# Two-layer decoder trunk on one core: where the norm between two parts is computed, and how the next part's weight splits queue around it

## The chip, the core and the metric

The kernel runs on one core of a Trainium2 chip, in one launch. The metric is device microseconds of that core, the median of several runs. The core has TensorE (PE, with its weight loads PEld), VectorE (DVE), ScalarE (ACT), GpSimd (POOL) and the DMA queue of SyncE (SP), each of which works through its own instructions in order.

## The reference, cut to what matters

The trunk has six parts in a row. Each normalizes its input, computes something with large weights, normalizes the result and adds it to x:

```python
def rmsnorm(x, g):
    y = x * lax.rsqrt(jnp.mean(x * x, -1, keepdims=True) + EPS)
    return y * g

def macaron_half_ffn(x, pre_g, post_g, w_gate, w_up, w_down):
    h = rmsnorm(x, pre_g)
    h = (jax.nn.silu(h @ w_gate) * (h @ w_up)) @ w_down
    return x + 0.5 * rmsnorm(h, post_g)

for p in layers:                       # two layers
    x = macaron_half_ffn(x, *p["ffn1"])
    x = x + rmsnorm(p["mixer"](rmsnorm(x, pre_g), *p["mix"]), post_g)
    x = macaron_half_ffn(x, *p["ffn2"])
```

x is 256 tokens by 1024 channels, float32; the FFN is 2816 wide. The mixer of layer 0 is sparse attention with a short convolution, that of layer 1 a recurrent time mixing.

## The kernel before, in words

Tokens lie on the 128 partitions, so x is two tiles, m = 0 (tokens 0 to 127) and m = 1. Every float32 product is made of three matmuls of rounded pieces (`mm3`, L265 to L270): an operand is split into a high piece (a copy on ACT) and a low piece (source minus high, on DVE or POOL). Weights are loaded by SP into one of four `raw` buffers and split by `split_u` (L214 to L233): the high piece of 128x1024 on ACT at L227, the low piece at L232 on DVE, or, for every `share`-th piece, in two halves of 128x512 on POOL. The pieces lie in 18 buffers `u`, two to a piece.

Each part ends in `out_proj` (L336 to L390). TensorE first finishes the output of m = 0 in two halves of 512 channels; `post_norm` (L317) takes each half: a Square with its row sum on ACT (L326), a multiplication by the gain on DVE (L328), and after the second half `rstd` (L273): the two sums and the epsilon are added on DVE (L276), the power -1/2 is taken on POOL (L277), and DVE adds the scaled halves to x (L331). Then `after(0)` starts the next part for m = 0: `pre_norm` (L282) makes the squares of x on ACT (L288), x times the gain (L290) on POOL for m = 0 and on DVE for m = 1, again `rstd`, and the multiplication by its result on DVE (L293). Eight transposes on TensorE (L300) follow, and `hT_split` splits what they give (L211 on ACT, L212 on DVE). The first FFN of all has no gain at this place (it multiplies later), so L290 isn't in it.

While this chain runs for m = 0, TensorE works on the output of m = 1: 15 of its last 16 steps of three matmuls may go ahead of the transposes of m = 0, the last step may not (`PIN`, L381). Then TensorE has the next part's first matmuls on m = 0, and behind them the transposes of m = 1, whose chain ran in the meantime.

The order within each engine is not written out: a scheduler that simulates the program orders the traced instructions and inserts waits. `issue_after(i)` adds one constraint to that: what is traced inside it stays behind instruction i on i's engine. The five ends of a part are called here A (first FFN to layer 0's mixer), B (that mixer to the second FFN), C (second FFN to the third), D (third FFN to layer 1's mixer) and E (that mixer to the last FFN).

The change touches `split_u`, `rstd`, `pre_norm` and `post_norm`. The three lines of the code that a sentence can't say so well:

```python
(nc.vector if m else nc.gpsimd).tensor_tensor(xg[:, sl], self.x[m][:, sl], g[:, sl], op=ALU.mult)      # L290
nc.vector.scalar_tensor_tensor(r, ss[0], eps, ss[1], op0=ALU.add, op1=ALU.add)                        # L276
nc.gpsimd.tensor_tensor(r2, r, self.nhalf, op=ALU.pow)                                                # L277
```

Of the kernel before, what the change touches and what calls it, by code (L numbers as in the profile page):

```python
# [8 lines left out]
F32 = mybir.dt.float32  # L9
F32R = mybir.dt.float32r  # L10
AF = mybir.ActivationFunctionType
ALU = mybir.AluOpType
# [3 lines left out]
P = 128  # L16
# [5 lines left out]
EPS = 1e-6  # L22
# [7 lines left out]
class Trunk:  # L30
# [31 lines left out]
    def __init__(self, tc, A, es):  # L62
        self.tc, self.nc, self.A = tc, tc.nc, A
        pool = lambda name, bufs, **kw: es.enter_context(tc.tile_pool(name=name, bufs=bufs, **kw))
        self.const = pool("const", 1)
        self.nlo = 0
        self.lead = None
        self.raws = pool("raws", 4)
        self.up = pool("up", 18)
        self.bp = pool("bp", 8)  # L70
        self.xp = pool("xp", 4)
        self.small = pool("small", 1)
        self.gains = pool("gains", 2)
        self.ps_mm = pool("ps_mm", 4, space=PSUM)
        self.ps_fl = pool("ps_fl", 2, space=PSUM)
        self.ps_tr = pool("ps_tr", 2, space=PSUM)
        self.ident = self.const.tile([P, P], F32, name="ident")
        make_identity(self.nc, self.ident)
        self.nhalf = self.const.tile([P, 1], F32, name="nhalf")
        self.nc.vector.memset(self.nhalf, -0.5)  # L80
        self.x = [self.const.tile([P, D], F32, name=f"x{m}") for m in range(2)]


# [128 lines left out]
        return self.nc.vector.tensor_sub(lo, src, hi.bitcast(F32))  # L212

    def split_u(self, src):  # L214
        n = src.shape[1]
        hi, lo = (self.u(F32R)[:, :n * src.shape[2]].rearrange("p (a b) -> p a b", a=n) for _ in range(2))
        self.nlo += 1
        if n == 1 and src.shape[2] == 512:

            if self.nlo % 3 == 0:  # L220
                self.nc.vector.tensor_copy(hi, src)
                self.nc.gpsimd.tensor_sub(lo, src, hi.bitcast(F32))
            else:
                self.split(src, hi, lo)
            return hi, lo
        pool = self.share and self.nlo % self.share == 0
        self.nc.scalar.activation(hi, src, AF.Copy)  # L227
        ax = 1 if n > 1 else 2
        m = src.shape[ax] // (2 if pool else 1)
        for i in range(0, src.shape[ax], m):  # L230
            c = (slice(None),) * ax + (slice(i, i + m),)
            (self.nc.gpsimd if pool else self.nc.vector).tensor_sub(lo[c], src[c], hi[c].bitcast(F32))  # L232
        return hi, lo  # L233
# [36 lines left out]
        mm(out, a[1], b[0], start=False, stop=stop)  # L270


    def rstd(self, ss, eps):  # L273
        nc = self.nc
        r, r2 = self.sm("rstd", 1, bufs=8), self.sm("rstd2", 1, bufs=8)
        nc.vector.scalar_tensor_tensor(r, ss[0], eps, ss[1], op0=ALU.add, op1=ALU.add)  # L276
        nc.gpsimd.tensor_tensor(r2, r, self.nhalf, op=ALU.pow)  # L277
        return r2

    HALF = (slice(0, 512), slice(512, 1024))  # L280

    def pre_norm(self, m, g=None):  # L282
        nc = self.nc
        xn, xg = self.xn(), self.x[m] if g is None else self.xn()
        ss = []
        for sl in self.HALF:
            ss.append(self.sm("ss", 1, bufs=8))
            nc.scalar.activation(xn[:, sl], self.x[m][:, sl], AF.Square, scale=1.0 / 32, accum_out=ss[-1])  # L288
            if g is not None:
                (nc.vector if m else nc.gpsimd).tensor_tensor(xg[:, sl], self.x[m][:, sl], g[:, sl], op=ALU.mult)  # L290
        r = self.rstd(ss, EPS)
        for sl in self.HALF:
            nc.vector.tensor_scalar(xn[:, sl], xg[:, sl], r, None, op0=ALU.mult)  # L293
        return xn
# [22 lines left out]
    def post_norm(self, m, g, half):  # L317

        nc = self.nc
        c = 0.5 if half else 1.0  # L320
        t, sq, ss = self.xn(), self.xn(), []

        def take(b):
            sl = self.HALF[len(ss)]
            ss.append(self.sm("ss", 1, bufs=8))
            nc.scalar.activation(sq[:, sl], b, AF.Square, scale=1.0 / (32 * c), accum_out=ss[-1])  # L326
            r = self.rstd(ss, EPS / (c * c)) if len(ss) == 2 else None
            nc.vector.tensor_mul(t[:, sl], b, g[:, sl])  # L328
            if r is not None:
                for sl in self.HALF:  # L330
                    nc.vector.scalar_tensor_tensor(self.x[m][:, sl], t[:, sl], r, self.x[m][:, sl],  # L331
                                                   op0=ALU.mult, op1=ALU.add)
        return take
# [1176 lines left out]
```

## Time and profile before

| what | value |
|---|---|
| runs | 1164.0, 1166.74, 1168.51 us (median 1166.74) |
| the profiled execution's own time | 1168.6 us |
| its span, first to last instruction | 1166.9 us |
| mean granted TensorE clock | 0.974 |
| busy: PE, DVE, ACT, POOL | 94%, 60%, 51%, 38% of the span |

The span is 1.7 us shorter than the time of the same execution, and that time lies 1.9 us above the median of the runs. A granted clock of 1.0 is 2.4 GHz, 0.5 is 1.2 GHz. A timeline row gives the start, the duration, engine, line, operation, what is written and read, and in brackets how long the engine had been idle and what ended that. Where a row says x2 or x4, several instructions in a row are merged.

### The profile page before, as it was taken

The numbers are of one execution on the slowest core, as the hardware profiler recorded it, in microseconds if no ns is written. First come the engines' busy times: TensorE is split into PE (matmuls) and PEld (weight loads), VectorE is DVE, ScalarE is ACT, GpSimd is POOL, SyncE is SP. The second block draws the span as 40 slices with busy tenths as digits, with TensorE's granted clock in tenths as the row PEclk, the third lists the DMA queues.
The fourth block names the chain that finished last, engine by engine and source line by source line (L and its number), as shares of the span: only waits on it lengthen the run. The fifth ranks groups of instructions, "written<-read, shape, count | busy, mean of one in ns | idle before, by whom it ended". The sixth has DMA issues, their size and how long they took to land. (4 is left out here: it accounts for less than half of the span.)

```text
span 1166.9 us, 16783 instructions
## 1 busy us (share of the span) xinstructions
PE 1098.3 (94%) x6429; PEld 924.2 (79%) x6429; DVE 705.3 (60%) x1165; ACT 594.4 (51%) x1106; POOL 446.3 (38%) x400
## 2 busy tenths in 40 slices
PE   6999998999979999998999999987889798999997
PEld 5888886888958888887888888776548776888886
DVE  5655525656886555427655543889894886655531
ACT  6655544245745555434655532557644454655540
POOL 3523234232563332324432433334463644432331
PEclk9999999999999999999999999999997888999999
DMA  9765562542464665555656563442312234765530
GB/s 324 253 216 180 182 212 64 166 145 73 152 207 154 215 210 182 181 179 180 196 168 196 182 201 106 145 145 73 108 37 92 92 129 142 227 205 179 182 108 36
DMA packets 130749, 187.46 MB, mean 161 GB/s; under 512 B 6871, under 2 KB 101087, under 8 KB 130670
## 3 DMA queue, kind: packets, MB, share of 16 engines
q1 hardware_dynamic: 130670, 186.41, 49.0%
q8 instruction: 50, 0.82, 0.3%
q14 instruction: 29, 0.24, 0.1%
HBM read 185.34 MB, written 1.05 MB: 160 GB/s over the span
## 5 line engine op out<-in xcount | busy, mean ns | idle before, releaser
L232 POOL TENSOR_TENSOR u<-raw,u 128x512 fp32r<-128x512 f32 x222 | 322.2, 1473 | 489.1 <-ACT u L227 476.1
L227 ACT ACTIVATE u<-raw 128x1024 fp32r<-128x1024 f32 x312 | 327.7, 1058 | 283.3 <-PE mm L269 79.7
L232 DVE TENSOR_TENSOR u<-raw,u 128x1024 fp32r<-128x1024 f32 x201 | 276.7, 1381 | 212.4 <-ACT u L227 211.9
L404 PE MATMUL mm<-b,u 128*128 128x512 f32 x504 | 181.3, 398 | 0.0
L404 PE MATMUL fl<-b,u 128*128 128x512 f32 x504 | 180.7, 397 | 0.0
L405 PE MATMUL fl<-b,u 128*128 128x256 f32 x504 | 141.5, 281 | 0.0
L405 PE MATMUL mm<-b,u 128*128 128x256 f32 x504 | 141.4, 280 | 0.0
L270 PE MATMUL fl<-u,b 128*128 128x512 f32 (+1 forms) x304 | 120.0, 396 | 4.8 <-DVE b L212 4.2
L268 PE MATMUL fl<-u,b 128*128 128x512 f32 (+1 forms) x304 | 120.5, 399 | 2.5 <-DVE u L780 1.4
L269 PE MATMUL fl<-u,b 128*128 128x512 f32 (+1 forms) x304 | 120.2, 395 | 1.5 <-DVE u L232 1.5
L268 PE MATMUL mm<-u,b 128*128 128x512 f32 (+1 forms) x296 | 114.8, 389 | 0.2 <-ACT u L211 0.2
L269 PE MATMUL mm<-u,b 128*128 128x512 f32 (+1 forms) x296 | 113.1, 384 | 1.1 <-DVE u L212 0.9
L270 PE MATMUL mm<-u,b 128*128 128x512 f32 (+1 forms) x296 | 112.5, 382 | 0.0
L404 PEld LDWEIGHTS fl<-b,u 128*128 128x128 f32 x504 | 94.9, 188 | 19.7
L404 PEld LDWEIGHTS mm<-b,u 128*128 128x128 f32 x504 | 94.8, 188 | 19.7
L405 PEld LDWEIGHTS mm<-b,u 128*128 128x128 f32 x504 | 95.2, 189 | 3.4
L405 PEld LDWEIGHTS fl<-b,u 128*128 128x128 f32 x504 | 95.2, 189 | 3.1
L270 PEld LDWEIGHTS fl<-u,b 128*128 128x128 f32 x304 | 58.9, 194 | 17.8 <-DVE b L212 4.8
L268 PEld LDWEIGHTS fl<-u,b 128*128 128x128 f32 x304 | 59.0, 194 | 16.2 <-ACT b L211 2.2
L269 PEld LDWEIGHTS fl<-u,b 128*128 128x128 f32 x304 | 59.0, 194 | 13.2 <-DVE u L232 1.7
L268 PEld LDWEIGHTS mm<-u,b 128*128 128x128 f32 (+1 forms) x296 | 55.9, 190 | 12.4 <-issue 1.1
L269 PEld LDWEIGHTS mm<-u,b 128*128 128x128 f32 (+1 forms) x296 | 55.9, 190 | 12.3 <-DVE u L212 1.2
(312 smaller groups left out, 1834.4 us busy)
## 6 DMA issues: line engine op xcount, KB each, us to landing
raw<-in_l_ffn_w_up_dram SPq DMA_DIRECT2D x44, 1024.0 KB, 5.3
raw<-in_l_ffn_w_down_dram SPq DMA_DIRECT2D x44, 1024.0 KB, 5.0
raw<-in_l_ffn_w_gate_dram SPq DMA_DIRECT2D x42, 1024.0 KB, 5.2
raw<-in_l_w_in_dram SPq DMA_DIRECT2D x9, 1024.0 KB, 6.8
raw<-in_l_w_v_dram SPq DMA_DIRECT2D x6, 1024.0 KB
raw<-in_l_w_out_dram SPq DMA_DIRECT2D x4, 1024.0 KB
raw<-in_l_w_r_dram SPq DMA_DIRECT2D x4, 1024.0 KB, 5.2
raw<-in_l_w_k_dram SPq DMA_DIRECT2D x4, 1024.0 KB, 5.2
```

The costliest lines, as they stand in the source:

```text
L227: self.nc.scalar.activation(hi, src, AF.Copy)
L232: (self.nc.gpsimd if pool else self.nc.vector).tensor_sub(lo[c], src[c], hi[c].bitcast(F32))
L268: mm(out, a[0], b[0], start=start, stop=False)
L269: mm(out, a[0], b[1], start=False, stop=False)
L270: mm(out, a[1], b[0], start=False, stop=stop)
L404: mm(b2, w[k][0], x, start=k == 0, stop=False)
L405: mm(b2[:, 0], w[k][1], x[:, 0], start=False, stop=False)
```

## The change

For m = 0 the multiplication of x by its gain goes to DVE too. The two halves' sums are added on ACT, as an Identity activation of the second sum whose bias is the first; the epsilon is added to the first sum on DVE as soon as that sum is there. This holds for both norms and both m. After the norm of m = 0 the last square (ACT), the last multiplication by the gain (DVE) and the power (POOL) are noted, and the weight splits traced after it, from the fifth piece on, must stay behind these three on their engines. Two small constants are set at the start and read by nothing.

```diff
+        self.tail_of, self.held, self.free = {}, [], 0
...
     def split_u(self, src):
+        self.free -= 1
+        with ExitStack() as es:
+            for i in self.held if self.free < 0 else ():
+                es.enter_context(self.tc.issue_after(i))
+            return self.split_free(src)
+
+    def split_free(self, src):
         n = src.shape[1]
...
-    def rstd(self, ss, eps):
+    def rstd(self, ss):
         nc = self.nc
         r, r2 = self.sm("rstd", 1, bufs=8), self.sm("rstd2", 1, bufs=8)
-        nc.vector.scalar_tensor_tensor(r, ss[0], eps, ss[1], op0=ALU.add, op1=ALU.add)
-        nc.gpsimd.tensor_tensor(r2, r, self.nhalf, op=ALU.pow)
+        nc.scalar.activation(r, ss[1], AF.Identity, bias=ss[0])
+        self.tail_of["pow"] = nc.gpsimd.tensor_tensor(r2, r, self.nhalf, op=ALU.pow).ins
         return r2
+
+    def sum_in(self, ss, sq, src, scale, eps):
+        s = self.sm("ss", 1, bufs=8)
+        i = self.nc.scalar.activation(sq, src, AF.Square, scale=scale, accum_out=s)
+        if not ss:
+            e = self.sm("sse", 1, bufs=8)
+            self.nc.vector.tensor_scalar(e, s, eps, None, op0=ALU.add)
+            s = e
+        ss.append(s)
+        return i
...
         for sl in self.HALF:
-            ss.append(self.sm("ss", 1, bufs=8))
-            nc.scalar.activation(xn[:, sl], self.x[m][:, sl], AF.Square, scale=1.0 / 32, accum_out=ss[-1])
+            self.tail_of["sq"] = self.sum_in(ss, xn[:, sl], self.x[m][:, sl], 1.0 / 32, EPS).ins
             if g is not None:
-                (nc.vector if m else nc.gpsimd).tensor_tensor(xg[:, sl], self.x[m][:, sl], g[:, sl], op=ALU.mult)
-        r = self.rstd(ss, EPS)
+                self.tail_of["xg"] = nc.vector.tensor_tensor(xg[:, sl], self.x[m][:, sl], g[:, sl], op=ALU.mult).ins
+        r = self.rstd(ss)
+        if m == 0 and g is not None:
+            self.held, self.free = list(self.tail_of.values()), 4
...
-            ss.append(self.sm("ss", 1, bufs=8))
-            nc.scalar.activation(sq[:, sl], b, AF.Square, scale=1.0 / (32 * c), accum_out=ss[-1])
-            r = self.rstd(ss, EPS / (c * c)) if len(ss) == 2 else None
+            self.sum_in(ss, sq[:, sl], b, 1.0 / (32 * c), EPS / (c * c))
+            r = self.rstd(ss) if len(ss) == 2 else None
```

## Rows read from the trace of the kernel before

**Rows 1.** The profile page, busy time of an engine, its share of the span and its instructions.
```profile
PE 1098.3 (94%) x6429; PEld 924.2 (79%) x6429; DVE 705.3 (60%) x1165; ACT 594.4 (51%) x1106; POOL 446.3 (38%) x400
```

**Rows 2.** The waits of PE over the whole span: who waited for whom, us in total, how often, the longest.
```profile
PE tr L300 <- DVE xn L293: 16.1, 8, 5.2
...
PE fl L270 <- DVE b L212: 4.2, 2, 2.3
```

**Rows 3.** Windows: length, busy time (and instructions) of PE, PEld, DVE, ACT and POOL, granted clock, DMA share and GB/s. The first five run from the last matmul on m = 0's output to the last transpose of m = 1, for the ends A, C, B, D and E; the last four are the stretches of granted clock 0.5 in A, B, C and E.
```profile
187.27:215.29 28.02, 23.80 (x113) 19.25 (x111) 21.31 (x29) 14.48 (x31) 15.59 (x13) 0.94 0.62 177
526.29:555.46 29.17, 26.10 (x113) 20.64 (x111) 22.41 (x26) 14.34 (x26) 12.44 (x10) 0.94 0.54 180
336.02:363.66 27.64, 22.08 (x97) 17.79 (x95) 20.38 (x24) 13.94 (x25) 12.70 (x10) 0.88 0.52 169
718.92:739.69 20.77, 20.77 (x108) 16.12 (x107) 15.45 (x32) 7.24 (x20) 9.81 (x9) 1.00 0.03 5
957.47:987.22 29.75, 25.76 (x109) 20.72 (x107) 21.03 (x26) 15.70 (x27) 15.33 (x12) 0.89 0.51 167
205.13:208.54 3.41, 3.41 (x10) 2.63 (x9) 3.35 (x6) 0.70 (x3) 1.80 (x3) 0.50 1.05 290
345.08:351.91 6.83, 3.59 (x12) 2.96 (x13) 6.16 (x6) 1.67 (x3) 3.90 (x3) 0.50 0.62 197
543.05:546.46 3.41, 3.41 (x10) 2.65 (x9) 3.41 (x6) 0.00 (x0) 0.55 (x1) 0.50 0.94 311
969.72:976.55 6.83, 5.62 (x17) 4.50 (x18) 6.29 (x8) 3.66 (x6) 2.28 (x3) 0.50 0.53 167
```

**Rows 4.** The timelines of PE, DVE, ACT and POOL in end B, engine by engine.
```profile
348.00 1.09 PE L300 MATMUL tr<-ident,xn 128*128 128x128 f32 x4 [5.25 <-DVE xn L293]
...
337.78 2.46 DVE L331 SCALAR_TENSOR_TENSOR x<-xn,rstd,x 128x512 f32<-128x512 f32 x2
340.15 2.32 DVE L232 TENSOR_TENSOR u<-raw,u 128x1024 fp32r<-128x1024 f32 x1
342.39 1.23 DVE L276 SCALAR_TENSOR_TENSOR rstd<-ss 128x1 f32<-128x1 f32 x1
...
346.37 2.89 DVE L293 TENSOR_SCALAR xn<-xn,rstd 128x512 f32<-128x512 f32 x2 [0.45 <-POOL rstd L277]
...
340.27 0.63 ACT L288 ACTIVATE xn<-x 128x512 f32<-128x512 f32 x1 [0.74 <-DVE x L331]
...
337.94 3.44 POOL L232 TENSOR_TENSOR u<-raw,u 128x512 fp32r<-128x512 f32 x2 [0.20 <-ACT u L227]
341.35 3.49 POOL L290 TENSOR_TENSOR xn<-x,gain 128x512 f32<-128x512 f32 x2
344.79 1.54 POOL L277 TENSOR_TENSOR rstd<-rstd,nhalf 128x1 f32<-128x1 f32 x1
```

**Rows 5.** The timelines of PE, DVE and POOL in end E.
```profile
970.61 1.08 PE L300 MATMUL tr<-ident,xn 128*128 128x128 f32 x4 [3.66 <-DVE xn L293]
...
960.29 2.46 DVE L331 SCALAR_TENSOR_TENSOR x<-xn,rstd,x 128x512 f32<-128x512 f32 x2
...
966.09 1.21 DVE L232 TENSOR_TENSOR u<-raw,u 128x1024 fp32r<-128x1024 f32 x1
...
968.98 2.89 DVE L293 TENSOR_SCALAR xn<-xn,rstd 128x512 f32<-128x512 f32 x2 [1.08 <-POOL rstd L277]
...
963.87 4.57 POOL L290 TENSOR_TENSOR xn<-x,gain 128x512 f32<-128x512 f32 x2
968.39 0.56 POOL L277 TENSOR_TENSOR rstd<-rstd,nhalf 128x1 f32<-128x1 f32 x1
```

**Rows 6.** The timeline of DVE in end C (the first four rows) and in end A (the last two).
```profile
528.04 1.42 DVE L331 SCALAR_TENSOR_TENSOR x<-xn,rstd,x 128x512 f32<-128x512 f32 x2
529.37 4.56 DVE L232 TENSOR_TENSOR u<-raw,u 128x1024 fp32r<-128x1024 f32 x2
...
534.66 2.93 DVE L293 TENSOR_SCALAR xn<-xn,rstd 128x512 f32<-128x512 f32 x2 [0.66 <-POOL rstd L277]
...
541.97 0.68 DVE L212 TENSOR_TENSOR b<-tr,b 128x512 fp32r<-128x512 f32 x1
...
197.66 2.88 DVE L293 TENSOR_SCALAR xn<-xn,rstd 128x512 f32<-128x512 f32 x2 [0.46 <-POOL rstd L277]
...
203.93 1.28 DVE L212 TENSOR_TENSOR b<-tr,b 128x512 fp32r<-128x512 f32 x2
```

**Rows 7.** Durations of one instruction: line L290 on POOL and on DVE (ns: least, median, most), and the group of ACT's smallest plain activations (us in all, mean ns).
```profile
L290 POOL TENSOR_TENSOR xn<-x,gain x10: 1267/1912/2318, 191.5 to 966.1; 128x512 f32<-128x512 f32 x10
L290 DVE TENSOR_TENSOR xn<-x,gain x10: 625/685/689, 208.4 to 981.1; 128x512 f32<-128x512 f32 x10
...
L960 ACT ACTIVATE pk<-pk 128x8 f32<-128x8 f32 x3 | 0.7, 227 | 0.1
```

**Rows 8.** The chain of m = 1 in ends A and C: windows (columns as in Rows 3) from the last matmul on m = 1's output to the first transpose of m = 1, and the multiplications on DVE that release these transposes.
```profile
201.95:214.25 12.30, 10.39 (x49) 8.71 (x49) 9.21 (x18) 3.76 (x9) 4.61 (x5) 0.86 1.06 290
539.00:554.42 15.42, 12.91 (x48) 9.87 (x48) 10.66 (x16) 3.72 (x9) 3.05 (x3) 0.89 0.79 270
...
210.41 0.88 DVE L293 TENSOR_SCALAR xn<-xn,rstd 128x512 f32<-128x512 f32 x2 [0.67 <-POOL rstd L277]
...
549.44 0.88 DVE L293 TENSOR_SCALAR xn<-xn,rstd 128x512 f32<-128x512 f32 x2 [0.66 <-POOL rstd L277]
```

More of the change, by code (lines that the diff above doesn't have):

```diff
@@ L80, in __init__ @@
         self.nc.vector.memset(self.nhalf, -0.5)
+        self.epsc = {}
+        for e in (EPS, EPS / (0.5 * 0.5)):
+            self.epsc[e] = self.const.tile([P, 1], F32, name="eps")
+            self.nc.vector.memset(self.epsc[e], e)
+        self.tail_of, self.held, self.free = {}, [], 0
         self.x = [self.const.tile([P, D], F32, name=f"x{m}") for m in range(2)]
```

## The prediction

> **What bounds the kernel now.** I read the page first: PE is busy for 94% of the span, no other engine for more than 60% [rows 1]. So time is won only where PE stands idle or runs slower than it could. The waits of PE come next: the longest entry is the transposes of the norm, which wait for the multiplication at L293 on DVE, 16.1 us in 8 waits, and the next of interest is the low split of what they give, 4.2 us in two waits [rows 2]. Then the windows around the five ends: PE's length minus its busy time is 4.22 us in A, 3.07 in C, 5.56 in B, 0.00 in D and 3.99 in E, 16.84 us together [rows 3]. Beside that stands a second loss: in A, B, C and E the granted clock falls to 0.5, the 1.2 GHz level, during or just after the idle time, and PE is busy for 3.41 + 3.59 + 3.41 + 5.62 = 16.03 us at that level [rows 3]. At 2.4 GHz the same work takes half, so 8.0 us hang on the same waits. What the change can reach is therefore 16.84 + 8.0 = 24.8 us, and D, which has no wait, gives nothing.
>
> The timelines say why L293 is late. In B, x is ready at 340.24 and its second square ends at 340.90, but POOL begins the multiplication by the gain only after a weight split, at 341.35, needs 3.49 us for it, and the power stands behind it until 346.33; the sum before the power waits on DVE behind a weight split of 2.32 us [rows 4]. E is the same: POOL multiplies from 963.87 to 968.44, and the power follows [rows 5].
>
> **The change part by part.**
> *The gain moves to DVE.* Five times two instructions of 1.9 us (median) leave POOL and cost 0.69 us each on DVE [rows 7]. On the chain of m = 0 that is 3.8 us out and 1.4 in; DVE's weight splits lose a neighbour too: in C the two took 4.56 us beside that POOL work, where one alone takes 1.21 [rows 5, 6].
> *The sums go to ACT.* 24 additions on DVE become 24 activations; the nearest row is 0.23 us for 128x8 [rows 7]. They are no longer behind weight splits on DVE, as in B, where the sum stood from 340.9 to 343.6 [rows 4], but may be behind one copy on ACT. The extra epsilon addition on DVE runs while ACT makes the second square, and I cost it at nothing; if DVE is in a weight split then, ACT's queue (its copies and the high splits) stands still with it, at most the 2.3 us of one split. The first norm and the last one have no gain to move: zero, plus or minus 0.2.
> *The hold.* It adds no instruction and no DMA; SP's issues stay where they are and only follow the later release of a `raw` buffer. It keeps the fifth and later pieces off the chain, but the four free ones may still stand in it, and the held ones may slip in between the gain and L293, while DVE waits for the power. I count one weight split there, 1.2 us alone or 2.3 beside POOL [rows 4, 5].
>
> What wait is left, end by end:
> - A: the chain gets 3.8 - 1.4 = 2.4 us shorter, and the transposes waited 4.22 - 1.9 = 2.3: gone. The low split (1.9, the wait of rows 2 that isn't the longest) stood on DVE until 203.93 [rows 6]; between 0 and 1.9 I take 0.6, nearer to B and E, where no such wait shows.
> - B: x ends at 340.24, the gain at 341.6, the one weight split at 342.8 to 343.9, the first half of L293 (0.5 alone, 2.0 of its 2.9 for two beside POOL) at 343.3 to 345.9. PE is free at 348.00 - 5.25 = 342.75. Taken: 2.0. Ends: 0 without a split; 4.2 if the gain takes the 2.46 us that the update of x took beside POOL.
> - C: gain to 530.8, two splits of 1.2 to 533.2, so L293 starts before its present 534.66; the 0.7 us outside the low split go. Of the low split's 2.3 (541.97, [rows 6]) I keep 0.8 as in A; ends 0 and 2.3.
> - E: x ends at 962.75, the gain at 964.1, the power is out by 964.5 since POOL is free at 963.87, a split to 965.3 or 966.4, L293's first half to 965.8 or 968.4; PE is free at 970.61 - 3.66 = 966.95. Taken 0.9; ends 0 and 2.5, worked out as in B.
>
> That leaves 4.3 of 16.84, so 12.5 us are won. The lower clock goes with the idle time: 8.0 x 12.5 / 16.84 = 6.0.
> *What is late next* is the chain of m = 1. In A PE's cover for it is 12.30 us, of which 1.91 was idle and 1.7 low clock, so 8.7 stay, and its L293 ended 9.3 us after the start of that window; in C 15.42 shrinks to 11.2 against 11.3 [rows 8]. So up to 0.7 us comes back at A, and I charge 0.7 to each of the four ends for held splits that now fall on this chain: 2.8.
>
> **The sum**: 12.5 + 6.0 - 2.8 = 15.7 us. The profiled execution's 1168.6 (span 1166.9) becomes 1152.9; the runs' median lies 1.9 lower, and 1166.7 - 15.7 gives 1151.0, which I predict.
>
> **The rivals.**
> *Contention.* In B and E a free weight split runs on POOL just when x is ready, and beside it the update of x took 2.46 us for two instead of the 1.42 of C [rows 4, 5, 6]. If the gain and L293 pay that in full, B and E keep 4.2 and 2.5 us, 3.8 more, with 1.8 of clock: 10.1 won, 1156.6. For it: L293 took 2.9 us for two in all four ends with a wait. Against: the gain took 0.69 at most on DVE for m = 1. The Trainium skill, "SBUF — State Buffer", section "Who interferes with whom", states this as a rule: a DVE instruction with two SBUF inputs and a GpSimd one that reads SBUF exclude each other for a whole instruction. By that rule the moved multiplication, with x and gain both in SBUF, would wait out POOL's running split, and the time would be this rival's; the slower update of x agrees with it.
> *It doesn't do what it says.* The scheduler puts the order by its own times, and may leave the weight splits in front of the power, L293 and the low splits. Then 4.2 + 2.5 stay in B and E and 1.9 + 3.0 in A and C, 5.2 us are won with 2.5 of clock, and m = 1 takes 5.2 (1.3 an end) back: 2.5, about 1164. For it: in A and C the fourth piece ends near where it does today. Against: POOL's two long instructions go whatever the order.
> *Slower.* The held splits bunch up. On DVE, released by the gain, they stand in front of L293 while it waits for the power. Two contended ones (4.6 us) bring B's L293 to 341.6 + 4.6 = 346.2, where it is now (346.37): that is the point from which it decides. Three (6.9) make B 2.1, E 2.0 and C 3.0 us later than now; that is +7.1, 1174. Against: L293 is traced ahead of these splits, and `u` buffers come free only as the last matmuls on m = 1 go by.
>
> **How the numbers follow.** Forecast 0.60, contention 0.17, not as it says 0.15, slower 0.08. A measurement of this kernel can tell about 0.5%, 5.8 us, from no change: faster means under 1160.9, slower over 1172.6. The first two cases are faster (0.77), the third is the same (0.15), the fourth slower (0.08). The forecast's own bounds are all of it won, 1166.7 - 24.8 = 1141.9, and the contention's 1156.6; the range 1143 to 1163 takes in most of the first two and about half of the third.
>
> **What would show it.** Right: no L290 on POOL, twenty on DVE at about 0.7 us; no sum on DVE, 24 activations of about 0.2 us on ACT, and no more activation table loads than now; in B and E PE's idle time before the first transposes under 2.5 us; PE's idle sum over the five windows near 4 to 7 instead of 16.84; granted clock 0.5 gone at least from A and C. Wrong: the same idle time with another releaser (a low split L212, a weight piece, or m = 1's transposes); splits between the gain and L293 on DVE for more than 2.3 us; or waits removed here that come back inside the two mixers, where PE is not as tightly packed as in the FFNs.

## The result and the profile after

The changed kernel took 1161.62 us, median of 5 runs (1158.79 to 1162.91), beside 1166.74 of the kernel before; ratio 0.9949, interval 0.9928 to 0.9969. By this measurement it is 5 to 6 us faster, where I forecast 15.7. Two later measurements of the same kernel, 12 runs each, gave 0.9987 (0.9960 to 1.0015) and 0.9986 (0.9966 to 1.0005), and the kernel before against itself 0.9988 (0.9974 to 1.0002). So the gain is small, 1.5 to 6 us by the three ratios, and the two later ones by themselves can't be told from no change. Experiment 2 below had three slow executions, which its ratio and its mean leave out, and its trace is of one of them (1172.8 us).

The page of the changed kernel, busy time by engine; it answers to [rows 1]:

```profile
PE 1093.6 (94%) x6429; PEld 921.9 (80%) x6429; DVE 701.2 (61%) x1177; ACT 601.0 (52%) x1130; POOL 429.6 (37%) x390
```

The counts are those of the diff: POOL lost its ten multiplications, ACT gained 24 sums. PE has 4.7 us less busy time. PE's waits in the changed kernel (who waited for whom, us in total, times, longest); they answer to [rows 2]:

```profile
PE tr L326 <- DVE xn L319: 12.2, 6, 4.1
...
PE tr L326 <- DVE u L694: 3.4, 1, 3.4
...
PE fl L284 <- DVE b L218: 3.0, 3, 1.4
```

The wait that I wanted to remove fell from 16.1 us to 12.2, no more. Windows of the changed kernel, columns as in [rows 3]: the ends A, C, B, D and E, then the mixers of layer 0 and of layer 1:

```profile
186.46:211.50 25.04, 21.90 (x113) 18.20 (x111) 20.12 (x30) 15.88 (x35) 12.90 (x11) 1.00 0.69 191
525.37:552.04 26.67, 24.42 (x113) 19.42 (x111) 20.73 (x27) 15.52 (x30) 9.64 (x8) 1.00 0.59 197
335.26:362.76 27.50, 22.35 (x98) 17.70 (x96) 17.77 (x25) 14.81 (x29) 9.60 (x8) 0.94 0.56 185
715.49:736.50 21.01, 20.86 (x108) 16.21 (x107) 16.23 (x33) 8.30 (x24) 6.89 (x7) 1.00 0.04 8
952.22:979.15 26.93, 24.80 (x109) 19.94 (x107) 20.98 (x29) 16.76 (x31) 11.35 (x10) 0.94 0.62 208
211.50:335.26 123.76, 117.16 (x832) 108.62 (x832) 82.14 (x221) 59.20 (x135) 41.75 (x39) 0.96 0.38 126
736.50:952.22 215.72, 185.03 (x1552) 144.72 (x1550) 179.58 (x368) 116.06 (x331) 104.17 (x132) 0.93 0.31 103
```

PE's idle time (length minus busy) is now 3.1 in A, 2.3 in C, 5.2 in B, 0.2 in D and 2.1 in E: 12.8 us where there were 16.84 and where I forecast 4.3. The ends took 135.3 us and take 127.2: they did get 8.2 us shorter, about half of that from the clock, which is at 1.00 in A and C. The same two mixers before:

```profile
215.29:336.02 120.73, 114.97 (x832) 105.59 (x833) 82.95 (x220) 59.62 (x135) 43.92 (x39) 0.99 0.40 131
739.69:957.47 217.78, 187.29 (x1550) 147.11 (x1550) 177.48 (x369) 115.93 (x331) 104.46 (x132) 0.92 0.33 106
```

Layer 0's mixer became 3.0 us longer, 0.8 of it idle time and the rest a clock of 0.96 instead of 0.99. In the second measurement of the changed kernel the two mixers were longer still:

```profile
212.07:342.78 130.71, 124.30 (x832) 115.87 (x832) 81.00 (x221) 59.20 (x135) 40.72 (x39) 0.90 0.37 119
744.04:964.59 220.55, 189.94 (x1552) 148.13 (x1551) 180.69 (x370) 116.40 (x331) 103.76 (x132) 0.91 0.32 105
```

That execution's ends took 126.2 us, as short as the first's, and its span was 1170.4. Both mixers together took 338.5 and 338.6 us in the two traces of the kernel before, and 339.5, 351.3 and 347.4 in the three of the changed kernel: in the first 1.0 us went back of what the ends had given, in the other two all of it. So two questions: why the ends kept 12.8 us of idle time, and why the mixers took back what the ends gave.

**Where the chain stands now.** End B of the changed kernel, timelines of ACT, POOL, DVE and PE; they answer to [rows 4]:

```profile
335.95 0.19 ACT L297 ACTIVATION_READ_ACCUMULATOR xn<-fl 128x1 f32 x1
336.04 1.05 ACT L241 ACTIVATE u<-raw 128x1024 fp32r<-128x1024 f32 x1
336.99 0.28 ACT L290 ACTIVATE rstd<-ss,sse 128x1 f32<-128x1 f32 x1
...
342.90 1.04 ACT L241 ACTIVATE u<-raw 128x1024 fp32r<-128x1024 f32 x1
343.85 0.28 ACT L290 ACTIVATE rstd<-ss,sse 128x1 f32<-128x1 f32 x1
...
337.17 2.52 POOL L246 TENSOR_TENSOR u<-raw,u 128x512 fp32r<-128x512 f32 x2 [6.59 <-ACT u L241]
339.65 0.56 POOL L291 TENSOR_TENSOR rstd<-rstd,nhalf 128x1 f32<-128x1 f32 x1
344.20 1.41 POOL L291 TENSOR_TENSOR rstd<-rstd,nhalf 128x1 f32<-128x1 f32 x1 [3.98 <-ACT rstd L290]
...
340.25 1.41 DVE L356 SCALAR_TENSOR_TENSOR x<-xn,rstd,x 128x512 f32<-128x512 f32 x2 [3.38 <-POOL rstd L291]
341.58 1.29 DVE L314 TENSOR_TENSOR xn<-x,gain 128x512 f32<-128x512 f32 x2
...
345.65 0.88 DVE L319 TENSOR_SCALAR xn<-xn,rstd 128x512 f32<-128x512 f32 x2 [0.45 <-POOL rstd L291]
...
346.28 1.33 PE L326 MATMUL tr<-ident,xn 128*128 128x128 f32 x8 [4.06 <-DVE xn L319]
```

The multiplication by the gain does what I said: 1.29 us for two on DVE. But the chain is late before it starts. The last square of the post-norm is read at 336.14; its sum stands on ACT behind a weight copy until 336.99; while it waits, a weight split gets onto POOL (337.17, 2.52 us), and the power comes only at 339.65. From the square's end to the power it is 3.5 us. The pre-norm's sum stands behind other work again, a square of m = 1 and a copy: x's second square was read at 342.43, the sum is made at 343.85. L319 starts 10.39 us after the window opens, as late as L293 did before (10.35). End E, ACT and DVE:

```profile
960.84 0.30 ACT L290 ACTIVATE rstd<-ss,sse 128x1 f32<-128x1 f32 x1 [1.89 <-DVE sse L300]
...
959.47 1.21 DVE L246 TENSOR_TENSOR u<-raw,u 128x1024 fp32r<-128x1024 f32 x1
960.61 0.14 DVE L300 TENSOR_SCALAR sse<-ss 128x1 f32<-128x1 f32 x1
```

It answers to [rows 5]. Here ACT stood idle for 1.89 us for the epsilon, 0.14 us of work that DVE did behind the gain and a weight split. And A and C, POOL's timeline, two windows of the changed kernel:

```profile
192.62 3.91 POOL L246 TENSOR_TENSOR u<-raw,u 128x512 fp32r<-128x512 f32 x2 [0.63 <-ACT u L241]
196.49 1.27 POOL L291 TENSOR_TENSOR rstd<-rstd,nhalf 128x1 f32<-128x1 f32 x1
...
531.34 4.24 POOL L246 TENSOR_TENSOR u<-raw,u 128x512 fp32r<-128x512 f32 x2 [4.13 <-ACT u L241]
535.55 0.54 POOL L291 TENSOR_TENSOR rstd<-rstd,nhalf 128x1 f32<-128x1 f32 x1
```

The place that the gain left on POOL has in both ends been taken by one of the four free pieces, again in front of the power (experiment 7 holds these pieces, and the power comes early).

### The profile page after: what moved, and what is told of

It is laid out like the page before. It is cut to its first block, busy times and chain, and to the rows that moved or that the text cites. A ratio compares the mean times of both kernels' runs of the same rounds, so it can differ in the third digit from the quotient of the medians.

```text
span 1159.0 us, 16840 instructions
## 1 busy us (share of the span) xinstructions
PE 1093.6 (94%) x6429; PEld 921.9 (80%) x6429; DVE 701.2 (61%) x1177; ACT 601.0 (52%) x1130; POOL 429.6 (37%) x390
## 4 chain that ended last, share of the span: by engine, by line
PE 76%; DVE 15%; issue 4%; ACT 3%; POOL 1%; DMA 0%; SPq 0%; DVEq 0%; POOLq 0%; ACTq 0%
PE mm L429 10%; PE fl L429 10%; PE fl L284 7%; PE fl L282 6%; PE fl L283 6%; PE fl L430 5%; PE mm L430 5%; PE mm L282 5%; PE mm L284 5%; PE mm L283 5%; DVE u L246 3%; PE tr L326 2%; PE fl L433 1%; PE mm L433 1%; DVE xn L1220 1%
## 5 line engine op out<-in xcount | busy, mean ns | idle before, releaser
L246 DVE TENSOR_TENSOR u<-raw,u 128x1024 fp32r<-128x1024 f32 x201 | 272.7, 1362 | 210.5 <-ACT u L241 210.2
L284 PE MATMUL fl<-u,b 128*128 128x512 f32 (+1 forms) x304 | 118.4, 390 | 3.5 <-DVE b L218 3.0
L282 PE MATMUL fl<-u,b 128*128 128x512 f32 (+1 forms) x304 | 118.7, 393 | 2.6 <-DVE u L800 1.3
L283 PE MATMUL fl<-u,b 128*128 128x512 f32 (+1 forms) x304 | 118.4, 389 | 1.5 <-DVE u L246 1.5
L284 PEld LDWEIGHTS fl<-u,b 128*128 128x128 f32 x304 | 57.8, 190 | 16.9 <-DVE b L218 4.3
L282 PEld LDWEIGHTS fl<-u,b 128*128 128x128 f32 x304 | 58.0, 191 | 15.1 <-ACT b L217 2.0
L283 PEld LDWEIGHTS fl<-u,b 128*128 128x128 f32 x304 | 58.0, 191 | 12.9 <-DVE u L246 1.7
L282 PEld LDWEIGHTS mm<-u,b 128*128 128x128 f32 (+1 forms) x296 | 55.8, 189 | 11.8 <-issue 0.7
```

The lines of the kernel that those rows point to most:

```text
L282: mm(out, a[0], b[0], start=start, stop=False)
L283: mm(out, a[0], b[1], start=False, stop=False)
```

## The experiments

"The ends" below are the five windows together in the profiled execution, PE's idle time in brackets. Low-clock time of a run is twice (1 - mean granted clock) times its span; it costs about half of itself where PE is busy. Each ratio is to the kernel before on the same chip, but not all experiments ran on one chip. 14 is 11 once more, and 17 is 12 once more.

| kernel | ratio (95%) | ends, us | mean low-clock time, us |
|---|---|---|---|
| before, first and again | 1; 0.9988 (0.9974 to 1.0002) | 135.3 (16.8), 133.4 (16.6) | 64 |
| changed, three times | 0.9949, 0.9987, 0.9986 | 127.2 (12.8), 126.2 (13.3), 127.9 (12.6) | 52, 63, 64 |
| 1 all pieces held | 1.0014 (0.9994 to 1.0034) | 129.9 (17.4) | 69 |
| 2 epsilon on ACT | 0.9960 (0.9929 to 0.9992) | 125.1 (11.8) | 60 |
| 3 gain back on POOL | 1.0000 (0.9983 to 1.0017) | 133.9 (16.4) | 61 |
| 4 no hold | 0.9987 (0.9971 to 1.0002) | 128.4 (14.9) | 61 |
| 7 POOL's free pieces held | 0.9986 (0.9969 to 1.0002) | 131.0 (14.3) | 61 |
| 8 = 7 with 2 | 1.0010 (0.9994 to 1.0025) | 131.0 (13.8) | 62 |
| 9 before, gain on DVE | 0.9974 (0.9956 to 0.9991) | 128.2 (12.8) | 60 |
| 10 changed, low split first | 0.9939 (0.9912 to 0.9966) | 124.2 (11.0) | 59 |
| 11 = 10 with 7, twice | 0.9926 (0.9911 to 0.9940), 0.9927 (0.9903 to 0.9950) | 124.3 (12.0), 126.4 (11.6) | 59, 55 |
| 13 no DVE weight splits | 0.9944 (0.9924 to 0.9963) | 128.3 (12.1) | 70 |
| 12 = 9 with low split first, twice | 0.9860 (0.9837 to 0.9883), 0.9880 (0.9855 to 0.9905) | 120.5 (8.4), 120.5 (8.3) | 47, 47 |
| 15 = 10 without the hold | 0.9994 (0.9973 to 1.0015) | 123.8 (11.5) | 64 |
| 16 = 10 with the sums on DVE | 0.9887 (0.9864 to 0.9909) | 120.5 (8.3) | 45 |

**Is it the free pieces?** Experiment 1 holds all of them.

```diff
-            self.held, self.free = list(self.tail_of.values()), 4
+            self.held, self.free = list(self.tail_of.values()), 0
```

> The changed kernel with no free pieces: every weight split traced after the norm of m = 0 stays behind the last square, the last gain and the power. Theory: what is left of PE's waits at the ends is the free weight splits on POOL that stand in front of the power (4.2 us in C, 3.9 in A, and 2.5 in B in front of the power of the norm before) and on DVE in front of the last multiplication. Then PE's idle time falls from 3.1 to 1.5 or less in A, from 2.2 to 0.8 or less in C and from 5.1 to under 3 in B, and the time by 4 to 6 us against the changed kernel (1155.5 to 1157.5). Rival: the chain is late for the new step, the epsilon on DVE that ACT's sum waits for; then idle time in A, C and E stays within 0.5 us each. Rival 2: the held splits come too late, and PE waits for weights after the transposes: slower by 3 us or more.

In A and C the transposes no longer waited, but idle time rose to 17.4 us: 2.9 us in C for a weight piece that now came late, 3.7 in E for m = 1's transposes. The free pieces are needed, as matmuls on m = 0 eat them.

**Is it the epsilon?** Experiment 2 makes it on ACT.

```diff
-            self.nc.vector.tensor_scalar(e, s, eps, None, op0=ALU.add)
+            self.nc.scalar.activation(e, s, AF.Identity, bias=self.epsc[eps])
```

> The changed kernel with the epsilon added on ACT (a second small Identity activation) instead of DVE. Theory: ACT's sum waited for the epsilon on DVE behind the gain and a weight split, 0.75 us in A and 1.9 in E; both waits go, PE's idle time in E falls from 2.1 to 1 or less, in A by 0.5 or less since POOL's split stands in front of the power there, C stays; the time falls by 1 to 3 us (1158.5 to 1160.5). Rival, POOL's free splits alone set the end: E's idle time stays at 2.1.

One to three microseconds of the ends, idle time 11.8. E, the end where ACT had waited for DVE, did not get shorter (27.2). The epsilon on DVE was not free, but it is the small part: the ratio can't be told from the changed kernel's (0.9960 beside 0.9949 to 0.9987), and on top of experiment 7 the same edit gave nothing (experiment 8, 1.0010 beside 0.9986).

**What are the gain and the hold worth alone?** Experiment 3 puts the gain of m = 0 back on POOL, 4 drops the hold, 9 is the kernel before with only the gain on DVE.

```diff
# 3
-                self.tail_of["xg"] = nc.vector.tensor_tensor(...).ins
+                self.tail_of["xg"] = (nc.vector if m else nc.gpsimd).tensor_tensor(...).ins
# 4
-            for i in self.held if self.free < 0 else ():
+            for i in ():
# 9, against the kernel before
-                (nc.vector if m else nc.gpsimd).tensor_tensor(xg[:, sl], ...)
+                nc.vector.tensor_tensor(xg[:, sl], ...)
```

> The changed kernel with x times the gain for m = 0 put back on POOL, the sums on ACT and the hold kept. Theory: moving the gain is what gave the time at the ends, so 5 to 8 us come back as PE's idle time and lower clock: idle time of the four ends about 15 to 17 us instead of 12.6, time 1165 to 1169. Rival, the sums on ACT gave it: within 2 us of the changed kernel.

> The changed kernel without the hold: no split is constrained. The orders of the two differ only around end B. Theory: the hold is worth what it does in B, 0 to 2 us; A, C, E stay within 0.3 us of the changed kernel in PE's idle time. Rival: the hold is what kept the fifth and later pieces off the chain everywhere; slower by 4 us or more.

> The kernel before with nothing changed but x times its gain for m = 0 on DVE. Theory: this move alone gives most of what the ends won (135.3 to 127.2): 127 to 130 us for the five ends, ratio 0.993 to 0.998. Rival: it pays only with the sums on ACT, since the sum on DVE then stands behind the gain and the weight splits as well: ends 132 or more, ratio 0.998 to 1.002.

Without the gain on DVE nothing of the change is left (1.0000). The gain alone is worth 0.0026, 3.0 us, and makes the ends nearly as short as the whole change does (128.2 beside 126.2 to 127.9). The hold is worth 1.2 us in the ends, all in B (28.7 without it). Sums and hold together added nothing that can be told from the gain alone.

Experiments 4 and 9 differ in one thing, the sums (with their epsilon), and the chain shows it. When L319 starts (L293 in the kernel before and in 9, L315 in 16), in us after the window of its end opens:

| kernel | sums on | A | B | C | E |
|---|---|---|---|---|---|
| before | DVE | 10.4 | 10.4 | 8.4 | 11.5 |
| changed | ACT | 11.6 | 10.4 | 10.8 | 10.1 |
| 4 no hold | ACT | 11.6 | 13.6 | 10.8 | 10.1 |
| 9 before, gain on DVE | DVE | 8.5 | 8.4 | 10.7 | 10.4 |
| 10 changed, low split first | ACT | 11.6 | 9.5 | 9.8 | 9.6 |
| 16 = 10 with the sums on DVE | DVE | 8.5 | 7.2 | 9.8 | 9.5 |

With the sums on ACT the chain is 3.2 us later in A and 5.2 us later in B, and within 0.3 us in C and E. In time the two experiments are not told apart (0.9987 and 0.9974): in A of experiment 9 the transposes wait 0.6 us only, but the low split behind them stands behind weight splits on DVE and PE waits 2.4 us for it.

**POOL's free pieces behind the power.** Experiment 7, and 8 with the epsilon on ACT as well:

```diff
-            for i in self.held if self.free < 0 else ():
+            for i in self.held if self.free < 0 else self.held[:1]:   # the power
...
-            self.held, self.free = list(self.tail_of.values()), 4
+            self.held, self.free = [self.tail_of[n] for n in ("pow", "sq", "xg")], 4
```

> The changed kernel with one more rule: of the four free pieces, what runs on POOL stays behind the power; their copies on ACT and subtractions on DVE are still free. Theory: the power waited for a weight split on POOL, 4.2 us in C, 3.9 in A, 2.5 in B (the norm before); PE's idle time falls from 3.1 to 1.5 or less in A, from 2.2 to 0.8 or less in C, from 5.1 to 2.6 or less in B, E (2.1) stays within 0.5; the five ends get 5 to 7 us shorter than 127.2. Rival, that which took the time back when all splits were held: the splits come too late, PE waits for a weight piece or a low split in C and for m = 1 in E; then the ends stay within 2 us of 127.2 or get longer.

> Both: POOL's free pieces behind the power, and the epsilon added on ACT. Theory: the two waits are in series on one chain, so each pays where the other doesn't hide it: ends together 2 to 3 us shorter than with POOL's pieces held alone, about 118 to 121 us, and the time 4 to 8 us under the changed kernel's ratio to before (0.987 to 0.992). Rival: low splits and weight pieces take it back, ends 125 or more.

The power came early and C's transposes no longer waited, and the time did not move. End C of experiment 7, DVE and PE:

```profile
528.14 2.95 DVE L319 TENSOR_SCALAR xn<-xn,rstd 128x512 f32<-128x512 f32 x2 [1.05 <-POOL rstd L291]
531.01 4.54 DVE L246 TENSOR_TENSOR u<-raw,u 128x1024 fp32r<-128x1024 f32 x2
...
536.14 3.91 DVE L246 TENSOR_TENSOR u<-raw,u 128x1024 fp32r<-128x1024 f32 x2
539.97 1.27 DVE L218 TENSOR_TENSOR b<-tr,b 128x512 fp32r<-128x512 f32 x2
...
537.89 0.49 PE L283 MATMUL mm<-u,b 128*128 128x512 f32 x1 [2.74 <-DVE u L246]
540.70 0.79 PE L284 MATMUL fl<-u,b 128*128 128x512 f32 x1 [2.32 <-DVE b L218]
```

L319 starts 5.6 us after the window opens (at 522.54), in the changed kernel 10.75 us after (536.12 and 525.37). But POOL's splits now run beside DVE's, four of which take 8.5 us, and the low split of what the transposes gave stands behind them. The wait moved one step down the chain. That names the next candidate: the low split's place.

**The low split first.** Experiment 10 adds the last low split of m = 0 to what the fifth and later pieces wait for; 11 joins 10 and 7.

```diff
-                self.split(pt, hi, lo)                  # in hT_split
+                self.held += [self.split(pt, hi, lo).ins] * int(h and self.fresh)   # fresh: m = 0 after a norm with gain
```

> The changed kernel, where the held weight splits must also stay behind the low split of what the transposes of m = 0 give (DVE). Theory: the waits of PE for the low split (1.35 us in A, 1.1 in B, 0.6 in C, up to 0.5 in E) are DVE's weight splits in front of it; they go, 3 us of idle time over the ends, and nothing else grows by more than 1 us, since PE has 24 matmuls (5.5 us) on the four free pieces: ends 123 to 125. Rival: the weight pieces behind them are then late, and PE waits for these (u) by as much.

> The same with POOL's free pieces behind the power as well. There PE waited in C 2.7 us for a weight piece and 2.3 for the low split, in A 2.6 for the low split. Theory: DVE has more weight splits to do in this stretch than fit, because POOL's now run beside them (2.3 us instead of 1.2 each); the low split's waits go (A to 0.5 or less, C to 0.5 or less) but the weight piece's wait stays or grows: idle time over the five ends 9 to 12 us instead of 14.3. Rival, the two waits had one cause: both go, idle time 6 or less, ends about 118.

> The changed kernel with POOL's free pieces behind the power and the held ones behind the low split, a second time, beside the kernel with two edits only. Theory: its ends repeat at 124.2 within 1, and the ratio, 0.9926 at first, lies between 0.990 and 0.996 again. Rival: the first time was luck of the granted clock in the mixers: ratio 0.996 or more.

The ends come to 124.2 to 126.4 us and the ratio to 0.993 to 0.994 in three measurements. On one chip the changed kernel had 0.9986, experiment 10 0.9939 and experiment 11 0.9926, so 5 to 7 us are won by this order, and it is still far from 15.7 us. Experiment 13 takes the DVE weight splits away altogether: the first pieces after a norm are made without the low subtraction on DVE, which leaves 25 subtractions out.

> The changed kernel that leaves out a part of the computation: of the first eight weight pieces after each norm of m = 0, those whose low piece DVE makes have no subtraction, and the matmuls read the high piece twice (25 subtractions less, the same matmuls). Theory: what is left of PE's waits at the ends is DVE's weight splits, in front of L319 or of the low split; with them gone PE's idle time over the five ends falls from 12.8 to 5 or less, the ends from 127 to 116 or less, and the time by 8 us or more against the changed kernel. Rival: the chain itself (squares, sum, power, POOL's splits) is as long as PE's cover; then the idle time stays over 9.

I had expected the idle time to go, and it stayed at 12.1 us. In A, m = 1's transposes waited 4.3 us, since on ACT a weight copy waiting 5.3 us for its DMA stood ahead of the second square. So weight splits on DVE are not the whole cause.

**Sums or hold?** Experiment 12 goes back to the kernel before, moves the gain and puts the fifth and later pieces behind the low split; sums stay on DVE, and nothing waits for the power, the squares or the gain. 15 is 10 without that hold, 16 is 10 with the sums on DVE.

```diff
# 12, against the kernel before: L290 as in 9, and
+        self.free -= 1                                  # in split_u
...
+            for i in self.held if self.free < 0 else ():
+                es.enter_context(self.tc.issue_after(i))
...
+                low = self.split(pt, hi, lo).ins        # in hT_split
+                if h and self.fresh:                    # m = 0 after a norm with gain
+                    self.held, self.free = [low], 4
# 15, against 10
-            self.held, self.free = [self.tail_of[n] for n in ("pow", "sq", "xg")], 4
+            self.held, self.free = [], 4
# 16, against 10
-        nc.scalar.activation(r, ss[1], AF.Identity, bias=ss[0])
+        nc.vector.scalar_tensor_tensor(r, ss[0], eps, ss[1], op0=ALU.add, op1=ALU.add)
...
-            self.nc.vector.tensor_scalar(e, s, eps, None, op0=ALU.add)   # in sum_in
```

> The kernel before with two edits only: x times its gain for m = 0 on DVE, and the fifth and later weight splits on DVE behind the low split of m = 0; the sums stay on DVE, nothing is held on ACT and POOL. Theory: the two parts that paid are the move of the gain (128.2 us for the ends alone) and the order of the low split (3 us); ends 124 to 126, ratio 0.992 to 0.997. Rival: the low split's order pays only with the hold behind the squares and the power; ends 128 or more.

> The norm multiplication of the gain on DVE, the sums on ACT with epsilon on DVE as in the change, and the next part's fifth and later weight splits queued only behind m=0's low split of hT; no hold of POOL and ACT pieces behind the power, the squares and the gain. Theory, that moving the sums to ACT is what takes back: the five ends together stay at 124 to 126 us (the sum waits for the epsilon addition and stands behind copies), ratio to before 0.992 to 0.996. Rival, that the change's hold is what takes back: the ends come to about 120.5 us as in the kernel with the sums on DVE and no hold, ratio 0.986 to 0.989.

> The gain on DVE, the low split first and the change's hold of the pieces, but the halves' sums on DVE as before, with epsilon in the same instruction. If moving the sums is the cost, the five ends take 120 to 122 us and the ratio to before is 0.985 to 0.990. Rival, that the hold is the cost: the ends take 124 us or more and the ratio is 0.992 or more.

> The kernel before with the gain on DVE and the fifth and later weight splits behind m=0's low split, run once more on the same chip as the two others: ends 120.5 us within 1, ratio to before 0.983 to 0.990. Rival, that its 0.986 was a favourable clock in the mixers and not its order: ratio 0.992 or more.

Once the low split goes first, it is the sums that decide, and not the hold. With the sums on DVE the ratio is 0.986 to 0.989 with the hold or without; with the sums on ACT it is 0.994 with the hold and 0.999 without. 15 and 17 ran on one chip and differ in the sums alone: 0.9994 against 0.9880. So do 10 and 16, on two chips: 0.9939 against 0.9887. The hold by itself did no harm (0.9887 against 0.9880) and, with the sums on ACT, helped. Of the 13 and 6 us between these pairs the ends show 3.3 and 3.7; the rest goes with the low-clock time (64 against 47 us, 59 against 45), which the traces have mostly outside the ends. The sums on DVE without the low split first are experiment 9, 3.0 us in all. The changed kernel with its sums on DVE and nothing else different was not run. End B of experiment 10:

```profile
336.23 0.28 ACT L290 ACTIVATE rstd<-ss,sse 128x1 f32<-128x1 f32 x1
...
336.41 2.52 POOL L246 TENSOR_TENSOR u<-raw,u 128x512 fp32r<-128x512 f32 x2 [6.56 <-ACT u L241]
338.90 0.56 POOL L291 TENSOR_TENSOR rstd<-rstd,nhalf 128x1 f32<-128x1 f32 x1
...
344.67 1.07 PE L326 MATMUL tr<-ident,xn 128*128 128x128 f32 x8 [3.21 <-DVE xn L319]
```

and of experiment 16, where only the sums differ:

```profile
335.46 0.16 DVE L290 SCALAR_TENSOR_TENSOR rstd<-ss 128x1 f32<-128x1 f32 x1 [2.47 <-ACT xn L297]
...
336.30 2.45 DVE L352 SCALAR_TENSOR_TENSOR x<-xn,rstd,x 128x512 f32<-128x512 f32 x2
338.67 2.38 DVE L310 TENSOR_TENSOR xn<-x,gain 128x512 f32<-128x512 f32 x2
...
335.70 0.56 POOL L291 TENSOR_TENSOR rstd<-rstd,nhalf 128x1 f32<-128x1 f32 x1 [5.53 <-DVE rstd L290]
336.46 3.44 POOL L246 TENSOR_TENSOR u<-raw,u 128x512 fp32r<-128x512 f32 x2 [0.20 <-ACT u L241]
...
342.42 1.06 PE L322 MATMUL tr<-ident,xn 128*128 128x128 f32 x8 [1.14 <-DVE xn L315]
```

The window opens at 334.50 in the one and 334.54 in the other. DVE stood idle and made the sum 0.04 us after the square was read (335.42); the power ran at 335.70, ahead of the weight split. That is 3.2 us earlier than in experiment 10. The update of x and the gain then pay for the split beside them, 2.4 us a pair, and the transposes still start 2.25 us earlier.

**The mixers.** They are part of it. Both together took 336.3 to 338.6 us in the six traces with the sums on DVE (the kernel before twice, 9, 12, 16, 17) and 336.6 to 351.3 us in thirteen with the sums on ACT (all but that of experiment 2), over 338.6 in eleven of these. The sums are not the whole of it: layer 0's mixer took 118.7 us in experiments 3 and 7, with the sums on ACT, and 123.8, 130.7 and 124.9 in the changed kernel. PE's order in it differs too: the wait of its transposes for L694 (L669 in the kernel before) is 1.3 us in all six traces with the sums on DVE, 3.4 in the changed kernel and in experiments 4, 10 and 15, but 2.4 in 7 and 11 and 1.3 in 3. Over all runs the low-clock time is 45 to 47 us in experiments 12, 16 and 17 and 52 to 64 us in the changed kernel and experiments 2, 10, 11 and 15. The short low-clock times come with both the sums on DVE and the low split first (experiment 9, without the latter, has 60); through which wait of the mixers it comes is open.

**Repeats.** The changed kernel twice and the kernel before once more:

> The changed kernel once more, for a second profile. Theory: the five ends are set by the order of the instructions and repeat, 127.2 us together within 0.5, and PE's idle time in them 12.8 within 0.5; what varies from one execution to the next is the granted clock inside the two mixers (stretches at 0.5 of 10.2 us in the first mixer and 30.7 in the second before), by several us. The ratio to before lies between 0.992 and 0.999. Rival: the first mixer's loss of 3.0 us is part of the change's order; then its length is again 123 to 124 us.

> The changed kernel a third time. Theory: ends 126 to 127.5 us; the first mixer's stretches at clock 0.5 again 7 us or more, where the kernel before has 3.4, so that on the mean about half of the 8 us that the ends won is lost there; time 1.5 to 5 us under the kernel before beside it. Rival: the low clock of the two earlier profiles (10.2 and 27.3) was chance: 0 to 3.4, and the time 7 to 9 us under.

> The kernel before, run as the kernel under test, for a second profile. Theory: the five ends repeat (135.3 us within 1), the stretches of FFN too; the first mixer's stretches at granted clock 0.5 are few (3.4 us in the first profile), the second mixer's about 34. Rival: the mixers' clock is chance in this kernel as well; then one of the two is off by 10 us or more.

The ends repeat within 1.7 us in the changed kernel and within 2.0 in the kernel before, PE's idle time in them within 0.7 and 0.2; the kernel before against itself is within its interval of 1.

## Why the prediction was right or wrong

The direction was right in the first measurement, the size was not: 5.1 us by the medians, where the sum said 15.7.

**The step that failed** is "the chain gets 3.8 - 1.4 = 2.4 us shorter", and with it the list of what wait is left, end by end. L293 had started 10.4, 10.4, 8.4 and 11.5 us after its window opened in A, B, C and E; L319 starts after 11.6, 10.4, 10.8 and 10.1, so it is earlier in E alone. In A, B and C what idle time went is due to L319 itself, 0.9 to 1.9 us for two in place of 2.9, and in A and C to the low splits. PE's idle time is 3.1, 5.2, 2.3 and 2.1 us in A, B, C and E, against 0.6, 2.0, 0.8 and 0.9 in my sum: 12.8 us stay in the five ends, where I left 4.3. Two terms made the chain late, the sums on ACT and the free pieces on POOL, both below.

**What bounds the kernel** held. PE stayed the bound, and the idle time and the lower clock of the ends are where time can be won: experiment 12 takes the ends to 120.5 us and 8.4 of idle, and gains 14 to 16 us.

**The gain on DVE** cost what I said in B, C and D (0.68 us median, twenty of them) and freed POOL. In A and E it ran beside a POOL split and took 2.38 us for two, which is the contention rival's price. The Trainium skill, "SBUF — State Buffer", section "Who interferes with whom", says that a DVE instruction with two SBUF inputs contends with a GpSimd one that reads SBUF, and that the port pair they share is an exclusive lock; the trace agrees (2.38 us for two beside POOL, 1.29 alone in B). It did not decide: experiment 16 pays it in B and is faster there.

**The sums go to ACT** is the first of them. "They are no longer behind weight splits on DVE [...] but may be behind one copy on ACT": I priced the instruction (0.23 us; it takes 0.29) and charged nothing for its place. On ACT it stands behind a copy or, in E, waits for the epsilon, and the power loses its place on POOL to a weight split. I looked only at the sum that was late on DVE (B's pre-norm, [rows 4]) and not at the post-norm's sum in the same end, which an idle DVE made at 336.94, with the power at 337.18. End B of the kernel before, DVE and POOL:

```profile
336.94 0.16 DVE L276 SCALAR_TENSOR_TENSOR rstd<-ss 128x1 f32<-128x1 f32 x1 [2.45 <-ACT xn L326]
...
337.18 0.56 POOL L277 TENSOR_TENSOR rstd<-rstd,nhalf 128x1 f32<-128x1 f32 x1 [5.50 <-DVE rstd L276]
```

By experiments 4 and 9 the term is 3.2 us of the chain in A and 5.2 in B. With them on DVE, L293 starts 1.9 and 2.0 us earlier there than in the kernel before, near the 2.4 that I had put down. In time the term is 6 us with the low split first and the hold (0.9939 less 0.9887), 13 us without the hold, and 1.5 us, which is not clear of noise, where the low split keeps its place (4 against 9).

**The epsilon at nothing** was wrong in E (1.89 us of ACT) and A, but small: experiment 2.

**The hold: "I count one weight split there"** counted DVE alone. A weight split on POOL in front of the power (3.9 us in A, 4.2 in C, 2.5 in B, there in front of the post-norm's) was the larger one. In that respect the rival "it doesn't do what it says", at 1164, came nearest: the pieces stayed in front of the power, on POOL. Holding these too only moved the wait (experiment 7); the order that works puts the low split ahead of the held pieces.

**The low splits** of A and C were seen, with 0.6 and 0.8 us left; they kept 1.35 and 0.57. But B, for which I had none, has one of 1.09, so it is 3.0 us in place of 1.4. I missed that with their order changed and the sums left alone most of the forecast was there to be had.

**m = 1's chain**, charged with 2.8 us, cost nothing: its transposes don't wait in any end of the changed kernel.

**The clock**: I had 6.0 us back in the ends; low-clock busy time there fell from 16.0 to 6.8 us, which gives 4.6. But the mixers took 1.0 us back in that trace, and 12.8 and 8.9 in the two others, more than the ends had won there. I had put "waits removed here that come back inside the two mixers" among the signs of being wrong and gave it no price.

## What to carry to other kernels

A tiny instruction on a chain costs its place in two queues: its own engine's, and the next engine's, where other work gets in while it waits. Before you move one, read what stands ahead of it at each place where it occurs, above all where it was on time. Keep background work behind the last instruction of the chain that anything waits for, not behind one in the middle, and measure the parts of a combined edit by themselves: here one part hid most of what another gave. And follow the chain one step past the wait that you remove: in experiments 7 and 9 the next link, the low split, took what the earlier power had won.

## What the runs showed of the hardware

The granted clock can fall to 0.5, the 1.2 GHz level, after a stretch in which PE shows no idle time, and stay there for different times in executions of one kernel. The window of the fall at 230.9 in the changed kernel's first profile, and the one at 230.7 in its second:

```profile
230.89:234.30 3.41, 3.41 (x18) 3.41 (x17) 1.72 (x7) 0.81 (x4) 1.42 (x2) 0.50 0.65 195
```

```profile
230.71:254.60 23.89, 23.34 (x109) 23.04 (x109) 8.57 (x22) 7.02 (x13) 6.61 (x8) 0.50 0.43 132
```

In both PE had been busy without a gap from 218.0 up to the fall, in the last 4 us with 32 matmuls of 128x33, in two rows of 16, and four transposes of 128x128 between them. During the fall it was busy all of the 3.41 us, and 23.34 of 23.89. In the third execution the clock stayed at 1.0 at this place (226.8 to 231.8, PE busy throughout). What decides it is open. Over its 12 runs that kernel's low-clock time lay between 51 and 84 us and its time between 1159.1 and 1173.9, so a difference of 5 us between two profiles says little, and only many runs, or windows of the stretch that was changed, do.
